# Two-layer decoder trunk on one core: longer planner distances in the first layer's mixers, and the dense block's last down products in another order

## The chip, the cores and the metric

The kernel runs on one core of one Trainium2 chip. The metric is the device time of one execution in microseconds (us). Three runs of the kernel before gave 674.22, 690.02 and 671.63 us; their median is 674.22 us.

## The reference, cut to what matters

256 tokens of width 1024 go through two layers. In each layer one projection feeds three groups of heads, whose outputs are joined and projected back; then come a layer norm, a feed-forward block and another layer norm. The feed-forward block is a dense SwiGLU in the first layer and a top-2-of-8 mixture of experts in the second. All values are float32.

```python
for layer in range(2):
    u, rq, rk, rv, rg, sq, sk, sv = split(x @ w_in[layer])
    y_ssm = s5_mixer(u, ...)              # diagonal complex scan, gelu, gated unit, norm of each group
    y_ret = retention_mixer(rq, rk, rv, rg, ...)   # 8 heads: rotary q and k, decayed scores, norm, silu gate
    y_sb  = stick_breaking_mixer(sq, sk, sv, ...)  # 4 heads: exp(z - cumulative sums), norm
    x = layer_norm(ALPHA * x + concat(y_ssm, y_ret, y_sb) @ w_out[layer])
    f = swiglu(x) if layer == 0 else moe_swiglu(x)
    x = layer_norm(ALPHA * x + f)
```

## The kernel before

**Main products.** Every float32 weight tile is split into a high part (`wh`, ScalarE, line 376) and a low part (`wl`, VectorE, line 378, a few on GpSimd), and each product is made of three TensorE products (`mm3`). Five pairs of split tiles are held (`NHL`), and a tile of a later block is split when an earlier one is done. In layer 0 the input blocks come in the order sv, rv0, u, sq, sk, rq0, rq1, rk0, rk1, rv1, rg0, rg1. A block is 48 TensorE products over two weight tiles of 24; u begins with the 97th product, rq0 with the 241st, and the last one of rg1 is the 576th. Then comes the product with `w_out`, eight row tiles in the order `OUT_ORDER`, the first two of which take the scan mixer's output.

**Lanes.** The mixers are Python generators (`s5_pre`, `s5_main`, `sb_lane`, `ret_lane`) in a planner, the class `Lanes`. The main loop calls `L.tick(1300)` after every 12 products (another count in some blocks), which advances the planned time, and each lane whose time has come then writes its next step, in the order in which the lanes were added: `s5_pre`, `s5_main`, `sb_lane`, `ret_lane`. `yield 2600` so means that the next step is written two ticks, 24 products, later. The planner's numbers are distances in program order and no waits on the chip. TensorE takes its instructions in the order written, save that the tile framework may place a step some products later when by its own estimate the operands are not there. On the chip, an engine works through its queue in order.

**The mixers' steps.** `s5_pre` makes the scan's tables: the powers `xext` (lines 578 to 581), `vmat` (591 to 598), the bank `g` (608 to 611, 64 small products in the trace), `tmat` (614 to 623) and four groups of transposes for `wmat` (625 to 636); `while not pe_open[l]` holds `g` back until block sk is through. `s5_main` makes two banks from `wmat` (`bre` and `bim`, lines 666 to 669), works on VectorE and GpSimd up to the scan (673 to 693), takes the product with `vmat` (695 to 697), copies `yc` out in 16 pieces that alternate between VectorE and ScalarE (699 to 709), and ends with gelu, the `glu` product (715 to 717), sigmoid, a square, the product for its norm (727) and the split into `mT_h`, `mT_l` (732). `sb_lane` goes twice through scores, triangle products (`sb_s`), value products (`sb_a`) and norm (`hd_q`); `ret_lane` goes four times through scores, value products and norm. The functions of ScalarE that need a table are chained in the order written (`fn`).

Before `w_out` the kernel drains the lanes; by the planner's arithmetic only `ret_lane` is then left, and its last steps are written one behind the other.

**The dense block's end.** `DOWN_AFTER[9]` is `[16, 17, 18, 19]`: four row tiles of `ffn_w_down` are multiplied after the last gate and up products, first for tokens 0 to 127 and then for the others, in two column halves `h`. The operands of rows 18 and 19, `f_h` and `f_l` (lines 1075 to 1080), come from the last gate and up products. The layer norm of a token half follows its four row tiles.

Of the kernel before, what the change touches and what calls it, by code (L numbers as in the profile page):

```python
# [226 lines left out]
Y2 = 6000  # L227
Y3 = 2500
# [7 lines left out]
def trunk(ctx, tc, I, out, dbg=None, layers=2):  # L236
# [232 lines left out]
    def s5_pre(l, mp, q, E):  # L469
# [134 lines left out]
                        P["d"].unsqueeze(2).to_broadcast([128, 8, 32]), op=OP.mult)  # L604
        while not pe_open[l]:
            yield 500

        g = Bank()
        for p in range(8):
# [16 lines left out]
        for c in range(2):  # L626
            for h in range(2):
                b = Bank()
                for p in range(4):
                    b.tr(b.t[:, p * 128:(p + 1) * 128], X[:, c, 4 * h + p].rearrange("p a b -> p (a b)"), ident)  # L630
                dst = Wm[:, c, 4 * h:4 * h + 4, :].rearrange("p a b -> p (a b)")
                if h:
                    S.activation(dst, b.t[:], AF.Copy)
                else:
                    V.tensor_copy(dst, b.t[:])
                yield 300
        P.update(V=Vt, T=Tm, W=Wm, tab=tab, R=R)
        S5P[l] = P
        yield 0
# [21 lines left out]
    def s5_main(l, mp, U, mT_h, mT_l):  # L661
        while l not in S5P:
            yield 500
        P = S5P[l]
        tab, R, Wm, Vt, Tm = P["tab"], P["R"], P["W"], P["V"], P["T"]
        bre, bim, y = Bank(), Bank(), Bank()
        for b, c in ((bre, 0), (bim, 1)):
            for p in range(8):
                b.mm_cols(b.t[:, p * 64:(p + 1) * 64], Wm[:, c, p, :], U[:, p, :])
        tc_, ts_ = (tab[:, c, :, 0:64] for c in range(2))  # L670
        tm = mp.tile([128, 4, 512], F32, name="s5t", tag="t8")
        z = mp.tile([128, 2, 512], F32, name="s5z", tag="t4a")
        V.tensor_tensor(tm[:, 0], tc_, bre.t[:], op=OP.mult)
        V.tensor_tensor(tm[:, 3], ts_, bre.t[:], op=OP.mult)
        V.tensor_tensor(tm[:, 1], ts_, bim.t[:], op=OP.mult)
        V.tensor_tensor(tm[:, 2], tc_, bim.t[:], op=OP.mult)
        G.tensor_tensor(z[:, 0], tm[:, 0], tm[:, 1], op=OP.add)
        G.tensor_tensor(z[:, 1], tm[:, 2], tm[:, 3], op=OP.subtract)
        yv = y.t[:].rearrange("p (a b) -> p a b", a=8)
        for p in range(8):  # L680
            y.mm_cols(yv[:, p, :], Tm[:, p].rearrange("p a b -> p (a b)"), U[:, p, :])
        Rf = R.rearrange("p a b -> p (a b)")
        zs = mp.tile([128, 2, 512], F32, name="s5s", tag="t4b")
        for c in range(2):
            V.tensor_tensor_scan(zs[:, c], Rf, z[:, c], 0.0, OP.mult, OP.add)  # L685
        E_ = mp.tile([128, 2, 8, 64], F32, name="s5e", tag="t4a")
        Ef = E_.rearrange("p a b c -> p a (b c)")
        V.tensor_tensor(tm[:, 0], tc_, zs[:, 0], op=OP.mult)
        G.tensor_tensor(tm[:, 3], ts_, zs[:, 0], op=OP.mult)
        V.tensor_tensor(tm[:, 1], ts_, zs[:, 1], op=OP.mult)  # L690
        G.tensor_tensor(tm[:, 2], tc_, zs[:, 1], op=OP.mult)
        V.tensor_tensor(Ef[:, 0], tm[:, 0], tm[:, 1], op=OP.subtract)
        V.tensor_tensor(Ef[:, 1], tm[:, 2], tm[:, 3], op=OP.add)
        yield 11000
        for p in range(8):
            for c in range(2):
                y.mm_cols(yv[:, p, 1:64], Vt[:, c, p].rearrange("p a b -> p (a b)"), E_[:, c, p, 0:63])
        yield 500
        yc = mp.tile([128, 2, T], F32, name="s5y", tag="t2a")
        yp = y.t[:].rearrange("p (h q c) -> p h q c", h=2, q=4)  # L700
        dv = yc.rearrange("p h (c j) -> p h c j", j=4)
        for j in range(4):
            for q in range(4):
                src = yp[32 * j:32 * j + 32, :, q, :]
                dst = dv[32 * q:32 * q + 32, :, :, j]
                if (j + q) % 2:
                    S.activation(dst, src, AF.Copy)  # L707
                else:
                    V.tensor_copy(dst, src)  # L709
        dump(f"s5y{l}", yc)  # L710
        g = mp.tile([128, 2, T], F32, name="s5g", tag="t2b")
        fn(g, yc, AF.Gelu_apprx_tanh)
        yield 4000
        b = Bank()
        for m in range(2):
            for k in range(2):
                b.mm(b.t[:, m * T:(m + 1) * T], P["glu"][:, k, m * 128:(m + 1) * 128], g[:, k, :])
        sg = mp.tile([128, 2, T], F32, name="s5sg", tag="t2c")
        for m in range(2):
            fn(sg[:, m], b.t[:, m * T:(m + 1) * T], AF.Sigmoid, bias=P["glu_b"][:, m:m + 1])  # L720
        o = mp.tile([128, 2, T], F32, name="s5o", tag="t2a")
        V.tensor_tensor(o, g, sg, op=OP.mult)
        sq = mp.tile([128, 2, T], F32, name="s5q", tag="t2c")
        S.activation(sq, o, AF.Square)
        yield 2500
        b = Bank()
        rs = rms_rstd(mp, b, slice(0, 512), sq.rearrange("p a b -> p (a b)"), C["blk16"], "t2b", 1)
        for m in range(2):
            V.scalar_tensor_tensor(o[:, m], o[:, m], P["norm_w"][:, m:m + 1], rs[:, m * T:(m + 1) * T],
                                   op0=OP.mult, op1=OP.mult)  # L730
        dump(f"s5o{l}", o)
        split2(mT_h[:, 0:2, :], mT_l[:, 0:2, :], o)
        yield 0

    def sb_lane(l, mp, qT, kT, v, mT_h, mT_l):
        P = PV[l]
        for ct in range(2):
            zb = [Bank(), Bank()]
            for h in range(2):
                pr = slice(64 * h, 64 * h + 64)  # L740
                zb[h].mm(zb[h].t[:, 0:256], kT[pr, ct, 0:128], qT[pr, ct, :])
                zb[h].mm(zb[h].t[:, 256:384], kT[pr, ct, 128:256], qT[pr, ct, 128:256])
            sm = mp.tile([128, 2, 384], F32, name="sb_s", tag="h3", bufs=3)
            e = mp.tile([128, 2, 384], F32, name="sb_e", tag="h3", bufs=3)
            for h in range(2):
                z = zb[h].t[:, 0:384]
                S.activation(e[:, h], z, AF.Abs)
                fn(e[:, h], e[:, h], AF.Exp, scale=-1.0)
                fn(e[:, h], e[:, h], AF.Ln, bias=b_one)
                V.scalar_tensor_tensor(sm[:, h], z, 0.0, e[:, h], op0=OP.max, op1=OP.add)  # L750
                dv = sm[:, h].rearrange("p (b n) -> p b n", b=3)[:, 0:3:2, :]
                G.affine_select(dv, dv, pattern=[[0, 2], [1, 128]], compare_op=OP.is_gt, fill=0.0, base=0,
                                channel_multiplier=-1)
            yield Y2
            A = mp.tile([128, 2, 384], F32, name="sb_a", tag="h3", bufs=3)
            for h in range(2):
                z = zb[h]
                z.mm(z.t[:, 256:384], C["ntri"], sm[:, h, 256:384])
                z.mm(z.t[:, 0:256], C["ntri"], sm[:, h, 0:256])
                z.mm(z.t[:, 128:256], C["nones"], sm[:, h, 256:384])  # L760
                fn(A[:, h], z.t[:, 0:384], AF.Exp)
                dv = A[:, h].rearrange("p (b n) -> p b n", b=3)[:, 0:3:2, :]
                G.affine_select(dv, dv, pattern=[[0, 2], [1, 128]], compare_op=OP.is_gt, fill=0.0, base=0,
                                channel_multiplier=-1)
            yield Y3
            o = Bank()
            av(o, A, v, 2 * ct)
            sq = mp.tile([128, T], F32, name="hd_q", bufs=2)
            S.activation(sq, o.t[:, 0:T], AF.Square)
            yield 1000  # L770
            rs = rms_rstd(mp, o, slice(T, 2 * T), sq, C["blk64"], "hd_rs")
            on = mp.tile([128, T], F32, name="hd_o", bufs=2)
            V.scalar_tensor_tensor(on, o.t[:, 0:T], P["sb_w"][:, ct:ct + 1], rs, op0=OP.mult, op1=OP.mult)
            split2(mT_h[:, 6 + ct, :], mT_l[:, 6 + ct, :], on)
            dump(f"sb{l}{ct}", on)
            yield 0
# [6 lines left out]
    def ret_lane(l, mp, qT, kT, v, sg, mT_h, mT_l):  # L783
        P = PV[l]
        for ct in range(4):
# [15 lines left out]
            av(o, A, v[ct // 2], 2 * (ct % 2))  # L801
            sq = mp.tile([128, T], F32, name="hd_q", bufs=2)
            S.activation(sq, o.t[:, 0:T], AF.Square)
            yield 1000
            rs = rms_rstd(mp, o, slice(T, 2 * T), sq, C["blk64"], "hd_rs")
            on = mp.tile([128, T], F32, name="hd_o", bufs=2)
            V.scalar_tensor_tensor(on, o.t[:, 0:T], P["gn_w"][:, ct:ct + 1], rs, op0=OP.mult, op1=OP.mult)
# [199 lines left out]
    def ffn(l, fp):  # L1007
# [78 lines left out]
                    router_operands(l + 1, fp)  # L1086
                    pre[l + 1] = L.add(pre[l + 1])
            for t in range(2):
                for h in range(2):
                    for j in DOWN_AFTER[9]:  # L1090
                        down(j, (t,), (h,), last=False)
                pe_open[1] = t == 1
                LNL[t] = L.add(L.urgent(ln(t, acc[t], lnw[:, 0], lnw[:, 1], fp), t == 0))
                L.tick(0)
# [472 lines left out]
```

## Time and profile before

| what | value |
|---|---|
| median of three runs | 674.22 us |
| the profiled execution's own time | 674.3 us |
| its span, first to last instruction | 672.6 us |
| mean granted TensorE clock | 0.979 of full speed |
| TensorE busy | 632.4 us, 94% |
| VectorE busy | 371.5 us, 55% |
| ScalarE busy | 301.6 us, 45% |
| GpSimd busy | 167.1 us, 25% |

The share of busy time is a mean over stages. A matmul's end is modelled and overlaps with the next one, so that the distance of two starts, and not the listed duration, is what a product costs. In a line of the timeline the first number is the start in us from the span's start, the second the time to the end of the line's instructions, and the square bracket the time for which the engine stood idle before it, with the instruction that released it.

### The profile page before, as it was taken

To read this page: it belongs to the slowest core of one execution; us is meant where nothing else is said; L and a number is where in the kernel's file an instruction comes from. 1 tells how busy PE (TensorE), PEld (TensorE's weight loads), DVE (VectorE), ACT (ScalarE), POOL (GpSimd) and SP (SyncE) were. 2 spreads that over 40 slices of the span, in tenths; PEclk is the share of its full clock that TensorE was granted. 3 is DMA by queue.
4 is the path that set the end of the run, shared out by engine and by line. 5 is a ranking of instruction groups with operands and counts; after the bars stand their busy time and mean duration, and the time that the engine had idled before them with its cause. 6 is when DMAs were issued, how large, how long until landed. Compare 5 with 4: busy or idle time off the path is not lost.

```text
span 672.6 us, 14222 instructions
## 1 busy us (share of the span) xinstructions
PE 632.4 (94%) x5652; PEld 500.0 (74%) x5652; DVE 371.5 (55%) x617; ACT 301.6 (45%) x484; POOL 167.1 (25%) x195
## 2 busy tenths in 40 slices
PE   5979889999999999999899998999899999999992
PEld 5978778679899999999799988878655544445542
DVE  5999866568576555555587864764830240012216
ACT  5655589557344444444355579852412200211102
POOL 1651650369998000000150342200000000000001
PEclk9979999999999999999899999999799999999997
DMA  8845155338555555555335241684099999999961
GB/s 323 308 152 161 63 173 179 119 118 288 196 189 188 188 188 188 188 190 187 126 126 189 95 157 63 236 315 194 6 390 335 409 409 352 417 413 414 414 262 67
DMA packets 38309, 150.87 MB, mean 224 GB/s; under 512 B 4640, under 2 KB 4768, under 8 KB 38240
## 3 DMA queue, kind: packets, MB, share of 16 engines
q1 hardware_dynamic: 38096, 149.64, 61.0%
q8 instruction: 49, 0.80, 0.5%
q10 hardware_dynamic: 144, 0.26, 0.1%
q14 instruction: 20, 0.16, 0.1%
HBM read 148.84 MB, written 1.05 MB: 223 GB/s over the span
## 4 chain that ended last, share of the span: by engine, by line
PE 71%; DVE 10%; ACT 9%; issue 5%; POOL 2%; DMA 1%; SPq 0%; DVEq 0%; POOLq 0%; ACTq 0%
PE bank L281 69%; DVE wl L378 3%; ACT wh L376 2%; PE bank L290 2%; ACT r_sw L937 2%; DMA st<-in_w_in_dram 1%; ACT L273 1%; ACT s5y L707 1%; POOL wl L378 1%; ACT L268 1%; DVE s5s L685 1%; ACT rstd L273 1%; DVE s5y L709 1%; DVE tv L579 0%; DVE xext L581 0%
## 5 line engine op out<-in xcount | busy, mean ns | idle before, releaser
L378 DVE TENSOR_TENSOR wl<-st,wh 128x1024 fp32r<-128x1024 f32 (+1 forms) x121 | 156.5, 1296 | 95.5 <-ACT wh L376 95.4
L376 ACT ACTIVATE wh<-st 128x1024 fp32r<-128x1024 f32 (+3 forms) x131 | 136.0, 1045 | 120.8 <-PE bank L281 100.3
L281 PE MATMUL bank<-xth,wh 128*128 128x256 f32 x608 | 174.1, 286 | 0.0
L281 PE MATMUL bank<-xtl,wh 128*128 128x256 f32 x608 | 171.8, 283 | 0.0
L281 PE MATMUL bank<-xth,wl 128*128 128x256 f32 x608 | 171.5, 282 | 0.0
L281 PEld LDWEIGHTS bank<-xth,wh 128*128 128x128 f32 x608 | 115.0, 189 | 2.0 <-issue 0.9
L281 PEld LDWEIGHTS bank<-xth,wl 128*128 128x128 f32 x608 | 115.3, 190 | 0.7 <-issue 0.5
L281 PEld LDWEIGHTS bank<-xtl,wh 128*128 128x128 f32 x608 | 115.1, 189 | 0.8 <-issue 0.2
L281 PE MATMUL bank<-ch,xe 128*32 128x344 f32 (+1 forms) x1280 | 94.2, 453 | 0.0
L281 PEld LDWEIGHTS bank<-ch,xe 128*32 128x32 f32 x1280 | 40.9, 110 | 50.0 <-issue 49.3
L378 POOL TENSOR_TENSOR wl<-st,wh 128x1024 fp32r<-128x1024 f32 (+1 forms) x10 | 21.5, 2176 | 124.8 <-ACT wh L376 124.8
L281 PE MATMUL bank<-ch,hT 128*32 x720 | 52.3, 451 | 0.0
L281 PEld LDWEIGHTS bank<-ch,hT 128*32 128x32 f32 x720 | 23.1, 110 | 27.9 <-issue 27.9
L281 PE MATMUL bank<-wh,xth 128*128 128x256 f32 (+1 forms) x112 | 30.4, 312 | 6.9 <-ACT wh L376 6.8
L281 PE MATMUL bank<-wh,f_h 128*128 128x512 f32 x88 | 35.8, 407 | 0.0
L281 PE MATMUL bank<-wl,f_h 128*128 128x512 f32 (+1 forms) x88 | 35.7, 406 | 0.0
L281 PE MATMUL bank<-wh,f_l 128*128 128x512 f32 x84 | 33.9, 406 | 1.7 <-DVE f_l L415 1.7
L1475 DVE TENSOR_TENSOR hs<-m_s,bank 128x344 f32<-128x344 f32 x10 | 5.1, 513 | 54.6 <-PE bank L281 54.1
L1499 DVE SCALAR_TENSOR_TENSOR y<-bank,gs,y 128x344 fp32r<-128x344 f32 (+1 forms) x15 | 8.6, 573 | 46.1 <-ACT y L1498 46.0
L1498 ACT ACTIVATE y<-bank,gs 128x344 fp32r<-128x344 f32 (+1 forms) x15 | 8.2, 546 | 50.4 <-PE bank L281 50.1
L1473 POOL MEMSET hs<- 128x200 f32 x2 | 0.5, 264 | 120.6 <-PE bank L290 74.2
L281 PE MATMUL bank<-wh,xtl 128*128 128x256 f32 (+1 forms) x112 | 29.0, 300 | 0.2 <-DVE xtl L415 0.2
(304 smaller groups left out, 1013.9 us busy)
## 6 DMA issues: line engine op xcount, KB each, us to landing
st<-in_w_in_dram SPq DMA_DIRECT2D x47, 512.0 KB, 3.7
ch<-in_moe_w_gate_dram SPq DMA_DIRECT2D x32, 688.0 KB, 8.9
ch<-in_moe_w_up_dram SPq DMA_DIRECT2D x32, 688.0 KB, 7.6
ch<-in_moe_w_down_dram SPq DMA_DIRECT2D x24, 688.0 KB, 13.5
st<-in_ffn_w_down_dram SPq DMA_DIRECT2D x21, 512.0 KB, 3.3
st<-in_ffn_w_gate_dram SPq DMA_DIRECT2D x20, 512.0 KB, 3.2
st<-in_ffn_w_up_dram SPq DMA_DIRECT2D x20, 512.0 KB, 3.2
st<-in_w_out_dram SPq DMA_DIRECT2D x16, 512.0 KB, 3.8
```

The costliest lines, as they stand in the source:

```text
L268: chained(S.preload_act_table_set("natural_log_exp_and_others"))
L273: chained(S.activation(out, in_, func, **kw))
L281: PE.matmul(o, lhsT, rhs, start=part not in self.begun, stop=True, skip_group_check=True)
L290: PE.transpose(o, i, ident)
L376: S.activation(hv, st, AF.Copy)
L378: x = (G if on_pool else V).tensor_tensor(lv, st, hv.bitcast(F32), op=OP.subtract)
L685: V.tensor_tensor_scan(zs[:, c], Rf, z[:, c], 0.0, OP.mult, OP.add)
L707: S.activation(dst, src, AF.Copy)
L709: V.tensor_copy(dst, src)
L937: S.activation(sw[32 * i:32 * i + 32], bv[32 * (i ^ 1):32 * (i ^ 1) + 32], AF.Copy)
L1498: S.activation(y[:wb, 0, j, 0:w], a, AF.Copy, scale=gs[:wb, j:j + 1])
L1499: V.scalar_tensor_tensor(y[:wb, 1, j, 0:w], a, gs[:wb, j:j + 1], y[:wb, 0, j, 0:w].bitcast(F32), op0=OP.mult, op1=OP.subtract)
```

## The change

In layer 0 alone seven distances become longer: 2600 in front of the bank `g`, 1200 behind the transposes of `wmat`, 1300 between `bre` and `bim`, 2600 and 1000 in the second pass of `sb_lane` (in front of the triangle products and of the value products), and 1000 in front of the norms' products of `sb_lane` and of `ret_lane`. In the dense block's end the row tiles 16 and 17 are taken for both column halves, then 18 and 19 for both.

```diff
@@ s5_pre
         while not pe_open[l]:
             yield 500
+        if l == 0:
+            yield 2600
 
         g = Bank()
...
                 yield 300
+        if l == 0:
+            yield 1200
         P.update(V=Vt, T=Tm, W=Wm, tab=tab, R=R)
@@ s5_main
         for b, c in ((bre, 0), (bim, 1)):
+            if l == 0 and c:
+                yield 1300
             for p in range(8):
@@ sb_lane
-            yield Y2
+            yield Y2 + 2600 * (1 - l) * ct
             A = mp.tile([128, 2, 384], F32, name="sb_a", tag="h3", bufs=3)
...
-            yield Y3
+            yield Y3 + 1000 * (1 - l) * ct
             o = Bank()
             av(o, A, v, 2 * ct)
             sq = mp.tile([128, T], F32, name="hd_q", bufs=2)
             S.activation(sq, o.t[:, 0:T], AF.Square)
-            yield 1000
+            yield 1000 + 1000 * (1 - l)
@@ ret_lane
-            yield 1000
+            yield 1000 + 1000 * (1 - l)
@@ ffn
             for t in range(2):
-                for h in range(2):
-                    for j in DOWN_AFTER[9]:
-                        down(j, (t,), (h,), last=False)
+                for js in (DOWN_AFTER[9][:2], DOWN_AFTER[9][2:]):
+                    for h in range(2):
+                        for j in js:
+                            down(j, (t,), (h,), last=False)
```

## Rows read from the trace of the kernel before

**Rows 1.** Timeline of TensorE (PE), 19 to 52 us: main products, bank `g`, first scores.
```profile
19.96 0.28 PE L281 MATMUL bank<-xth,wh 128*128 128x256 f32 x1
...
38.45 0.28 PE L281 MATMUL bank<-xth,wl 128*128 128x256 f32 x1
41.16 0.31 PE L281 MATMUL bank<-prm,xext 128*64 128x32 f32 x4 [2.44 <-DVE xext L580]
42.05 0.31 PE L281 MATMUL bank<-cneg,xext 128*64 128x32 f32 x4 [0.58 <-DVE xext L581]
...
43.00 0.33 PE L281 MATMUL bank<-cneg,xext 128*64 128x32 f32 x4
...
45.21 1.66 PE L281 MATMUL bank<-sb_sq,sb_sk 64*128 64x256 f32 x8 [0.60 <-ACT sb_sk L921]
...
51.14 0.60 PE L290 MATMUL bank<-cst,xext 128*128 128x128 f32 x4
```

**Rows 2.** Busy time by stretch, granted clock (PEclk), DMA share, GB/s.
```profile
43.00:50.00 7.00, 6.40 (x57) 5.88 (x55) 6.83 (x13) 4.84 (x11) 0.79 (x2) 0.51 0.26 79
20.00:92.00 72.00, 61.80 (x643) 58.55 (x642) 68.39 (x104) 42.95 (x71) 42.26 (x51) 0.95 0.48 164
```

**Rows 3.** Timeline of ScalarE (ACT) at 44 us, the copy that the first scores need.
```profile
44.56 0.60 ACT L921 ACTIVATE sb_sk<-bank 128x512 f32<-128x512 f32 x1
```

**Rows 4.** Timeline of VectorE (DVE) at 45 us, the low part of rq0's second tile.
```profile
45.78 1.22 DVE L378 TENSOR_TENSOR wl<-st,wh 128x1024 fp32r<-128x1024 f32 x1
```

**Rows 5.** Timeline of TensorE, 62 to 125 us: mixers' products and the first of `w_out`.
```profile
62.06 1.15 PE L281 MATMUL bank<-s5u,wmat 128*64 128x64 f32 x32 [0.52 <-ACT tmat L621]
...
64.96 1.15 PE L281 MATMUL bank<-s5u,wmat 128*64 128x64 f32 x32 [1.08 <-ACT wh L376]
...
81.74 1.14 PE L281 MATMUL bank<-sb_s,cst 128*128 128x128 f32 x6 [2.47 <-POOL sb_s L752]
...
85.62 2.09 PE L281 MATMUL bank<-s5e,vmat 128*64 128x63 f32 x64
...
91.59 1.22 PE L281 MATMUL bank<-sb_a,sb_v 128*64 128x256 f32 x8 [2.28 <-POOL sb_a L763]
...
95.09 0.70 PE L281 MATMUL bank<-hd_q,cst 128*128 128x256 f32 x2 [0.67 <-ACT hd_q L769]
...
97.14 0.93 PE L281 MATMUL bank<-rrq,rrk 64*128 64x256 f32 x8
...
106.68 0.70 PE L281 MATMUL bank<-hd_q,cst 128*128 128x256 f32 x2 [0.95 <-ACT hd_q L803]
...
124.71 0.50 PE L281 MATMUL bank<-wh,mth 128*128 128x512 f32 x1
```

**Rows 6.** Timeline of VectorE, the scan mixer's low part for `w_out`.
```profile
114.90 0.69 DVE L415 TENSOR_TENSOR mtl<-s5o,mth 128x512 fp32r<-128x512 f32 x1
```

**Rows 7.** Timeline of ScalarE, 103 to 114 us: a table load, the sigmoid, the silu.
```profile
103.80 0.40 ACT L414 ACTIVATE mth<-hd_o 128x256 fp32r<-128x256 f32 x1
104.22 1.28 ACT L273 ACT_TABLE_LOAD   x1
105.52 0.84 ACT L273 ACTIVATE s5sg<-bank,small 128x256 f32<-128x256 f32 x2
...
113.54 0.60 ACT L273 ACTIVATE vg<-bank 128x512 f32<-128x512 f32 x1
```

**Rows 8.** Timeline of TensorE, 325 to 334 us: the dense block's last down products.
```profile
325.32 0.39 PE L281 MATMUL bank<-wh,f_h 128*128 128x512 f32 x1
...
326.49 0.40 PE L281 MATMUL bank<-wh,f_l 128*128 128x512 f32 x1
...
329.25 0.50 PE L281 MATMUL bank<-wh,f_l 128*128 128x512 f32 x1 [1.69 <-DVE f_l L415]
...
329.81 0.61 PE L281 MATMUL bank<-wl,f_h 128*128 128x512 f32 x1
...
333.20 0.42 PE L281 MATMUL bank<-wh,f_h 128*128 128x512 f32 x1
```

## The prediction

> **What bounds the kernel now.** I read the page first: TensorE is busy nearly throughout, so what can be won is its idle time and the stretches at the lower clock, where each product costs twice as much. The list of TensorE's waits came next, then its timeline wherever a wait of layer 0's mixers or of the dense block's end stood. Seven waits belong to the groups that the change moves away: 2.44 and 0.58 us in front of bank `g` [rows 1], 0.52 and 1.08 in front of `bre` and `bim`, 2.47 in front of the second triangle products, 2.28 in front of the second value products, 0.67 and 0.95 in front of two norms [rows 5]. An eighth, 1.69 us, is the down products' [rows 8]. Behind the first, the clock goes from 2.4 to 1.2 GHz: it stood at 0.51 of full in 43 to 50 us [rows 2]. The 155 main products from 19.96 to 38.45 us give 0.119 us for one at full speed [rows 1]. The last thing to see is that TensorE is not alone: VectorE was busy 68.39 of the 72 us from 20 to 92 [rows 2], so a product moved here may meet another late operand.
>
> **Where the steps go.** The planner's arithmetic, followed through yields and ticks, gives each step a place, counted in main products of the input blocks. Before and after: first scores of `sb_lane` 252 and 252, bank `g` 252 and 276, transposes 276 to 312 and 300 to 336, `bre` 324 and 360, `bim` 324 and 372, second scores 360 and 372, second triangle products 420 and 456, their value products 444 and 492, their norm 456 and 516, first retention scores 468 in both, first retention norm 504 and 516, product with `vmat` 432 and 480, `glu` 492 and 540, the scan mixer's norm 516 and 564. `w_out` follows the 576th in both. No instruction is added except one load of a ScalarE table, below; no DMA moves against another.
>
> **Part 1, bank `g`.** The wait of 2.44 + 0.58 us was for `xext`. With `g` 24 products later, the first scores are next. They need the copy of sk, which ScalarE ended at 44.56 + 0.60 = 45.16 us [rows 3], and rq0's second tile, the products behind the 264th, needs a low part that VectorE ended at 45.78 + 1.22 = 47.00 [rows 4]. Neither hangs on `g`; both queue behind `xext` and the copies of u, which the change leaves alone. So I take the idle time to stay and to be put down to `sb_sk` or `wl`, and the clock to fall as before. Passing the 264th at 47.0, TensorE does 12 products at the low clock, 12 x 0.238 = 2.9 us, then `g`, whose groups of four are 0.119 us apart (eight steps from 42.05 to 43.00) [rows 1], 16 of them 1.9 us at full speed: 51.7 us. Before, the same place, the first transposes, was reached at 51.14 [rows 1]. Cost 0.6 us. Bounds: with `g` still at the low clock another 1.9 us, 2.5 in all; if VectorE's queue is put in another order and nothing is late, a gain of 2.44 + 0.58 + 0.60 and of 7 x 0.49 = 3.4 us of clock, 7.0 in all.
>
> **Part 2, `bre` and `bim`.** Their 0.52 + 1.08 us go: `wmat`'s last transposes stand 24 products, 2.9 us, ahead of `bre` instead of 12. Gain 1.6, at least 0.
>
> **Part 3, the second pass of `sb_lane`.** Scores and triangle products are 84 products apart instead of 60: 2.9 us of cover against the 2.47 us. What is late there is VectorE's step at line 750, which stands behind the scan in the queue; the scan now starts where the scores do and can still stand before it. Gain 2.5, at least 0. The value products get 12 products and the first retention scores between, 1.4 + 0.9 us [rows 5], against 2.28; each norm 1.4 us against 0.67 and 0.95. Gain 3.9, at least 0.
>
> **Part 4, what is late next.** The scan mixer's end moves by 48 products towards `w_out`. From the `vmat` product to the first `w_out` product it was 124.71 - 85.62 = 39.1 us [rows 5]. Off go 48 x 0.119 = 5.7, the retention scores that now stand ahead of it, 0.9, and the 3.9 us of waits gained in part 3: 28.6 us are left. The mixer's own path, from the `vmat` product over copies, gelu, `glu`, sigmoid, square and norm to the split, took from 85.62 to 114.90 + 0.69, that is 30.0 us [rows 5, 6]. Its sigmoid is now written behind rg0's silu, and chained functions keep that order: one more table load, 1.28 + 0.02 us, and the silu's 0.60 [rows 7] come into the path, 31.9 us. So 3.3 us come back as a wait at `glu`, at the mixer's norm or at `w_out`. Bounds: none, if so much of the 30.0 us was waiting for other work of ScalarE and VectorE; 6.7, if the idle time lowers the clock for as long as in part 1 (3.4 us).
>
> For this load the Trainium skill (ScalarE: Activation LUTs, "What ACT_TABLE_LOAD costs") gives 2.66 us for a switch of table, the load and a drain of 1.38 us. The trace does not agree: the load began 0.02 us behind the end of the instruction before it and the sigmoid 0.02 us behind the load [rows 7]. By the page the path would be 1.4 us longer and the time, an estimate, 1.4 us above the forecast; I go by the rows.
>
> **Part 5, the down products.** From 325.32 to 326.49 five steps took 1.17 us, 0.234 each. The first `f_l` product that waits stood eighth behind 325.32 and was released at 329.25 [rows 8]. Now 14 products stand ahead of it, so TensorE reaches it at 325.32 + 14 x 0.234 = 328.6 and waits 0.65 us: 1.0 won. Behind the old wait eight products took 333.20 - 329.81 = 3.39 us where 8 x 0.234 = 1.87 do [rows 8], the lower clock; I take the shorter idle time not to lower it: 1.5 won. The layer norm's first half starts later, but its two VectorE steps still fit beside the last six products, 1.4 us, of the other half. Gain 2.5, between 0 (the operand later still) and 3.2.
>
> **The sum.** -0.6 + 1.6 + 2.5 + 3.9 - 3.3 + 2.5 = 6.6 us. All that comes behind, the experts' weight stream included, starts from these products and shifts with them. The profiled execution took 674.3 us, its span 672.6, within 0.1 of the median: 674.3 - 6.6 = **667.7 us**.
>
> **The rivals.**
> *The first stall goes too.* If copy and low part are placed earlier, part 1 gives 7.0 instead of -0.6: 660.1 us. For it: block sk's products were through before 38.45 us [rows 1], 6 us ahead of the copy. Against: nothing in the change touches what is queued ahead of them. Chance 0.13.
> *The waits only move.* VectorE, 68.39 of 72 us busy [rows 2], sets the pace up to 92 us, and each wait taken away turns up at another step; the mixers give nothing and part 5 alone stays: 671.8 us. For it: VectorE's share. Against: most waits lie at 81 us and later, with other engines' names on them. Chance 0.22.
> *The scan mixer's end becomes the path* (slower). Its in-order copies and table loads stand between the `vmat` product and `w_out`, now with 28.6 us of cover. If its path grows by 10 us over the 30.0, with new table switches and retention's squares in between, the wait is 13.3 and the lost clock 3.4, 16.7 instead of 3.3: 681.1 us. It decides the sign from a cost of 9.9 us on, which is a path of 35.1 with the clock lost. For it: the path runs over two engines that alternate 16 times. Against: part of the 30.0 was waiting for work that now comes earlier. Chance 0.08.
>
> **How the numbers follow.** The forecast has 0.57, the rivals 0.43. The worst ends of all parts together give -9.2 us, the best 18.2; they hardly meet. The range 661 to 674 holds the forecast and the second rival and leaves out the slow one and most of the first, under 2 in 10. Two per cent, about what a measurement of this kernel can tell from no change, is 13.5 us. Faster by more (under 660.8): half of the first rival and a little of the forecast, 0.09. Slower by more (over 687.7): 0.02. Within: 0.89.
>
> **What would show it.** Right: idle time in front of the first scores or of rq0's second tile at 39 to 47 us, with the clock at half up to about 50; no idle in front of `bre`, the second triangle products and the second norm; some microseconds at `glu`, the scan mixer's norm or the first `w_out` product; `w_out` beginning near 120.6 us instead of 124.7; full clock through the down products. Wrong: full clock at 43 to 50 us; no new wait from 95 to 125 us; or waits at the first retention scores, whose operands pass through the same full VectorE queue.

## The result, and the profile after

The changed kernel takes **678.7 us**, the median of four runs from 678.31 to 679.21, against 674.94 for the kernel before in the same job: 1.0078 times as long, 95% interval 1.0051 to 1.0104. Now and then an execution of any kernel takes some per cent longer (690.02 us among the four of the kernel before), and the ratios leave such executions out. The forecast was 667.7. The profiled execution took 678.31 us, its span 676.6, so 4.0 us more than the span before.

TensorE's timeline, layer 0's mixers and `w_out`; the rows answer to [rows 1, 5]:

```profile
44.98 1.66 PE L281 MATMUL bank<-sb_sq,sb_sk 64*128 64x256 f32 x8 [5.94 <-ACT sb_sk L927]
...
87.53 1.15 PE L281 MATMUL bank<-sb_s,cst 128*128 128x128 f32 x6 [3.48 <-POOL sb_s L758]
88.91 2.08 PE L281 MATMUL bank<-sb_s,cst 128*128 128x128 f32 x6 [0.23 <-POOL sb_s L758]
95.24 1.49 PE L281 MATMUL bank<-rrq,rrk 64*128 64x256 f32 x8 [2.31 <-POOL rrk L945]
...
120.42 1.12 PE L281 MATMUL bank<-s5q,cst 128*128 128x512 f32 x2 [2.28 <-ACT s5q L730]
127.33 0.50 PE L281 MATMUL bank<-wh,mth 128*128 128x512 f32 x1
...
144.85 0.50 PE L281 MATMUL bank<-wh,mth 128*128 128x512 f32 x1 [2.17 <-ACT wh L376]
146.11 0.50 PE L281 MATMUL bank<-wl,mth 128*128 128x512 f32 x1 [0.76 <-DVE wl L378]
```

Seven of the nine waits of [rows 1, 5] are gone. The other two have grown, at the first scores from 0.60 to 5.94 us and at the second triangle products from 2.47 to 3.48, and two new ones stand at the first retention scores (2.31) and the scan mixer's norm (2.28). Added up over every line from 36 us to the first `w_out` product, TensorE was idle for 11.83 us before (the nine waits and 0.24 us at 83.12) and for 14.24 now. The idle time has moved, and it has grown by 2.4 us. That product starts 2.6 us later (127.33 against 124.71). The windows show the clock, columns as in [rows 2]:

```profile
43.00:50.00 7.00, 5.02 (x24) 4.63 (x25) 6.83 (x14) 5.18 (x12) 0.56 (x2) 0.59 0.25 79
88.00:92.00 4.00, 3.77 (x17) 3.35 (x16) 2.91 (x4) 2.73 (x5) 1.17 (x2) 0.58 0.49 144
96.00:99.00 3.00, 3.00 (x17) 2.71 (x15) 2.27 (x3) 0.94 (x1) 3.00 (x4) 0.52 0.71 236
146.00:150.00 4.00, 3.89 (x10) 3.12 (x11) 1.45 (x3) 0.00 (x0) 3.84 (x9) 0.58 0.40 131
330.00:345.00 15.00, 14.46 (x78) 11.99 (x77) 11.58 (x16) 6.05 (x10) 5.08 (x3) 1.00 0.30 106
```

Behind the waits at 87.5 and 95.2 us the clock goes to its lower level, 1.2 GHz. In the trace of the kernel before it did not go down between 80 and 130 us. By the granted clock that costs 4 x 0.42 + 3 x 0.48 = 3.1 us of products. Idle time and clock together are 5.5 us, so 2.9 us must have come back elsewhere ahead of `w_out`: two norm products (0.6 us) now stand behind its first product and not ahead of it; the rest is not broken down.

From the first `w_out` product to the layer norm behind it another 4.6 us are lost: GpSimd's low parts there end at 163.42 against 156.23, 7.2 late. The idle time of that stage is 3.12 us against 0.79, the clock is low from 146 to 150 (4 x 0.42 = 1.7 us), and the two norm products make up the rest. Only the dense block gives something back:

```profile
336.46 0.50 PE L281 MATMUL bank<-wh,f_l 128*128 128x512 f32 x1 [0.54 <-DVE f_l L415]
```

The wait is 0.54 us instead of 1.69 [rows 8] and the clock stays at 1.00 from 330 to 345 us; before, eight products behind the wait took 3.39 us at the lower level [rows 8]. The lag goes from 7.2 to 4.0 us, which is the change of the span.

### The profile page after: what moved, and what is told of

Its sections match the earlier page's. It is cut to its first block, busy times and chain, and to the rows that moved or that the text cites. A ratio compares the mean times of both kernels' runs of the same rounds, so it can differ in the third digit from the quotient of the medians.

```text
span 676.6 us, 14231 instructions
## 1 busy us (share of the span) xinstructions
PE 632.5 (93%) x5652; PEld 501.5 (74%) x5652; DVE 369.4 (55%) x617; ACT 303.0 (45%) x485; POOL 168.8 (25%) x195
## 4 chain that ended last, share of the span: by engine, by line
PE 69%; DVE 10%; ACT 8%; issue 6%; POOL 4%; DMA 1%; SPq 0%; DVEq 0%; POOLq 0%; ACTq 0%
PE bank L281 68%; DVE wl L378 2%; ACT wh L376 2%; PE bank L290 2%; ACT r_sw L943 1%; DMA st<-in_w_in_dram 1%; POOL s5w L497 1%; ACT L273 1%; POOL wl L378 1%; ACT s5y L713 1%; POOL r_sw L944 1%; ACT L268 1%; ACT rstd L273 1%; DVE s5s L691 1%; DVE s5y L715 0%
```

## Where the waits went

VectorE's timeline of the changed kernel, 78 to 90 us: the scan, then `sb_s` (the operand of the second triangle products), then the rope step of rk0:

```profile
78.77 3.42 DVE L691 TENSOR_TENSOR_SCAN s5s<-rdec,s5z 128x512 f32<-128x512 f32 x2 [2.02 <-POOL s5z L683]
...
86.44 1.01 DVE L756 SCALAR_TENSOR_TENSOR sb_s<-bank,sb_e 128x384 f32<-128x384 f32 x2
...
88.51 0.67 DVE L941 TENSOR_TENSOR rrk<-rope,bank 128x512 f32<-128x512 f32 x1
```

The same steps before:

```profile
70.82 2.29 DVE L685 TENSOR_TENSOR_SCAN s5s<-rdec,s5z 128x512 f32<-128x512 f32 x1 [0.86 <-POOL s5z L677]
...
80.66 1.01 DVE L750 SCALAR_TENSOR_TENSOR sb_s<-bank,sb_e 128x384 f32<-128x384 f32 x2
```

Before, too, the scan stood ahead of `sb_s`, and rk0's rope step was at 82.72. With `bre` and `bim` 36 and 48 products later the scan starts 8 us later, and what stands behind it in the queue is 6 us later.

ScalarE's timeline, 140 to 146 us, in the `w_out` stage:

```profile
140.51 0.21 ACT L517 ACTIVATE s5w<-s5w 128x8 f32<-128x8 f32 x1 [3.84 <-POOL s5w L513]
...
143.74 1.79 ACT L376 ACTIVATE wh<-st 128x1024 fp32r<-128x1024 f32 x2
```

The weights' copies for TensorE stand behind layer 1's table functions, the first of which waits for GpSimd. The same functions stood there before:

```profile
133.86 0.21 ACT L517 ACTIVATE s5w<-s5w 128x8 f32<-128x8 f32 x1 [3.27 <-POOL s5w L513]
```

They are now 6.7 us later, `w_out` only 2.6.

## The experiments

Each time is compared with runs of the kernel before on the same chip, given as a ratio; by the job above the changed kernel has 1.0078. "Before +" and "after +" say which kernel was edited; the distances are called scan (in front of `g`, `bre`, `bim`) and heads (second pass of `sb_lane`, both norms).

**One part alone.** Before + the down order:

> The kernel before with the down products' new order alone. If this part did what its step in the prediction says, the wait of 1.69 us falls to about 0.5 and the clock stays up behind it: 2.5 to 3.3 us faster than before, near 671.5 us. If the order only moves the wait to the layer norm behind it: no difference.

0.9962 [0.9928, 0.9996], and 0.9951 [0.9932, 0.9971] in a second set:

> The new order of the down products alone, once more, on the same chip as the two versions with the vmat product 24 products later, to tell what of their gain is its own: 672 to 673.5 us by the term of 2.5 us. Theory (the distances are worth 1 to 2 us more): 1 to 2 us slower than the version with both. Rival (they are worth nothing): as fast as that.

Part 5 holds by itself, with 2.6 to 3.3 us. Before + the scan distances:

> The kernel before with the scan mixer's three distances alone (2600, 1200, 1300). Theory of the late scan: VectorE's long scan steps start some 8 us later and stand ahead of the second scores' step and of the rope steps in its queue, the mixer's end comes close to w_out, and the change's loss is all here: 6 to 11 us slower than before, 680 to 685 us. Rival, the late heads: the four longer distances of the heads do the harm by crowding the products near w_out: this kernel within 2 us of before.

1.014 [1.0088, 1.0191]: 9.5 us slower, more than the whole change. Its trace has the long wait behind the scan at another place than the changed kernel's. `sb_s` stands ahead of the scan here, and TensorE doesn't wait for it. But rk0's rope step on VectorE stands behind the scan's last additions, ScalarE's copies behind that step, and the second exponential of `sb_a` behind these copies, 8 us after its triangle products (ScalarE, then TensorE):

```profile
87.34 2.39 ACT L943 ACTIVATE r_sw<-bank 32x512 f32<-32x512 f32 x4 [6.15 <-DVE rrk L941]
89.76 0.49 ACT L273 ACTIVATE sb_a<-bank 128x384 f32<-128x384 f32 x1
```

```profile
91.50 1.54 PE L281 MATMUL bank<-sb_a,sb_v 128*64 128x256 f32 x6 [5.16 <-POOL sb_a L769]
```

Before + the head distances, then those with the down order:

> The kernel before with the four heads' distances alone (2600 and 1000 in the second pass of the stick-breaking lane, 1000 in front of the norms). Theory of the late scan: the scan steps stand early as before, the four waits of 2.47, 2.28, 0.67 and 0.95 us go: 3 to 6 us faster, 668 to 671 us. Rival, the late heads: 4 to 8 us slower.

> The changed kernel without the scan mixer's three distances. Theory of the late scan: both gains add, 6 to 9 us faster than before, 665 to 668 us. Rival, the late heads: about as slow as the changed kernel, 676 to 680 us.

1.0021 [0.998, 1.0063] and 0.997 [0.9935, 1.0004]. The heads win nothing alone, and with the down order no more than that order. The second of these is the changed kernel without the scan distances, so taking those out gives back some 7 us (0.997 against 1.0078). In the trace with the heads alone the removed waits come back, most of them at one place, `glu`: TensorE's idle time up to `w_out` is 11.95 us, as before, and the clock is 0.57 from 96 to 104 us. ScalarE's queue (first fence) and TensorE's (second):

```profile
97.54 0.39 ACT L707 ACTIVATE s5y<-bank 32x128 f32<-32x128 f32 x1 [0.45 <-DVE s5y L709]
97.94 1.28 ACT L273 ACT_TABLE_LOAD   x1
99.24 0.63 ACT L273 ACTIVATE s5g<-s5y 128x512 f32<-128x512 f32 x1
...
101.18 0.87 ACT L273 ACTIVATE sb_a<-bank 128x384 f32<-128x384 f32 x2
```

```profile
87.33 1.14 PE L281 MATMUL bank<-sb_s,cst 128*128 128x128 f32 x6 [1.05 <-POOL sb_s L752]
...
99.92 3.78 PE L281 MATMUL bank<-s5g,prm 128*128 128x256 f32 x8 [5.17 <-ACT s5g L273]
```

The exponentials of `sb_a` could start at 88.5 us, behind the triangle products. They start at 101.18, behind the copies of y and the gelu. Before, they ran ahead of these copies, which began at 92.15:

```profile
87.68 0.87 ACT L273 ACTIVATE sb_a<-bank 128x384 f32<-128x384 f32 x2
```

**Half of the scan distances.** Before + only `g`; before + only `bre` and `bim`:

> The kernel before with the longer distance in front of bank g alone (24 products). Theory (the scan goes late): the idle time in front of g only moves to the first scores (5.8 us behind the copy of sk, against 2.44 + 0.58 + 0.60 before), and the scan mixer's bre and bim move from the 324th to the 348th product, half of the way that all three distances move them. All three alone cost 9.2 us; so this one costs about half, 3 to 6 us: 678 to 681 us against 675, with the second triangle or value products waiting 2 to 5 us at 82 to 92 us. Rival 1 (only the bre/bim distances hurt): 675.5 us, the waits at 82 to 92 us as before, 2.47 and 2.28. Rival 2 (the distance of g carries all of it): 683 to 685 us.

> The kernel before with the two distances in front of bre and bim alone (12 products each: bre from the 324th to the 336th, bim to the 348th). Theory (the scan goes late): the 0.52 and 1.08 us in front of bre and bim go, the 2.44 + 0.58 + 0.60 us in front of g and the first scores stay; the scan starts some 2 to 3 us later and stands in VectorE's queue ahead of the second scores' step: the second value products wait 4 us or more instead of 2.28, the low clock behind them. 676 to 679 us against 675. Rival 1 (as the prediction had it, these waits are simply won): 673.4. Rival 2 (the distance of g is harmless and these two carry all 9.2 us): 683 to 685.

1.0141 [1.0091, 1.019] and 1.0163 [1.0108, 1.0218]. Either half costs as much as the whole, so my sharing out by products was wrong. With `g` alone the first scores wait 6.00 us, and the second triangle products:

```profile
86.86 3.79 PE L281 MATMUL bank<-sb_s,cst 128*128 128x128 f32 x12 [6.63 <-POOL sb_s L754]
```

With `bre` and `bim` alone TensorE's wait for `sb_s` is 7.39 us at 84.48, and VectorE shows its cause:

```profile
81.54 0.69 DVE L696 TENSOR_TENSOR s5e<-s5t 128x512 f32<-128x512 f32 x1
...
82.47 0.55 DVE L754 SCALAR_TENSOR_TENSOR sb_s<-bank,sb_e 128x384 f32<-128x384 f32 x1
```

In both, `bim` is at the 348th product, 12 in front of the second scores, and apart from one 0.42 us step the scan's end is the last that VectorE finishes ahead of `sb_s`. So a distance does not cost by its length: `sb_s` stands behind the scan before, in these two and in the changed kernel, with 2.47, 6.63, 7.39 and 3.48 us of waiting, and with all three scan distances alone it is `sb_a` that comes late. Much of the price is the clock: up to `w_out` TensorE's idle time is only 3.9 us (`g`) and 1.8 us (`bre` and `bim`) above the 11.83 before, but the clock was at half behind these waits (0.51 from 85 to 92 us; 0.50 from 80 to 90) and again near `w_out` (0.50 from 126 to 139; 0.51 and 0.50 from 124 to 134).

**The place in VectorE's queue.** After, with the scan emitted 12 products later:

```
         zs = mp.tile([128, 2, 512], F32, name="s5s", tag="t4b")
+        if l == 0:
+            yield 1300
```

> The changed kernel with the scan itself emitted 12 products later, so that the second scores' step (sb_s, first half) stands in VectorE's queue ahead of the scan's four multiplications and additions (82.12 to 86.44 us) and no longer behind them; the vmat product and the scan mixer's end go 12 products further. Theory (the scan went ahead of the second scores' step, and that is the wait of 3.48 us): this wait falls to under 1 us and the low clock behind it goes, 674 to 676.5 us against 678.7; what the scan mixer's end then lacks is at most 1.5 us. Rival (sb_s waits for POOL's select or ScalarE's exponentials, not for the scan): the wait stays over 2.5 us, 678 to 681.

1.0208 [1.0136, 1.028], far slower than either theory had it:

```profile
84.61 1.14 PE L281 MATMUL bank<-sb_s,cst 128*128 128x128 f32 x6 [1.55 <-POOL sb_s L760]
...
94.14 1.66 PE L281 MATMUL bank<-rrq,rrk 64*128 64x256 f32 x8 [3.72 <-POOL rrk L947]
123.23 2.08 PE L281 MATMUL bank<-s5q,cst 128*128 128x512 f32 x2 [5.39 <-ACT s5q L732]
...
129.72 0.50 PE L281 MATMUL bank<-wh,mth 128*128 128x512 f32 x1 [1.73 <-ACT mth L414]
...
145.07 0.93 PE L281 MATMUL bank<-rrq,rrk 64*128 64x256 f32 x8
```

The wait for `sb_s` falls from 3.48 to 1.55, with 0.73 in place of 0.23 at its second half, so the scan's place was its cause for the larger part. But the retention scores wait 3.72 us instead of 2.31: the two steps together cost 6.0 us, as in the changed kernel, and the idle time has moved once more.

The price is at `w_out`. With 12 products more the scan mixer is not done when the input blocks end. The kernel's `drain` in front of `w_out` (line 958 of the kernel before) then finishes that lane alone, with no products between its last steps: its norm waits 5.39 us and `w_out` 1.73. With no other lane left, as in the kernel before and the changed one, the same line writes out all of `ret_lane`; here the scores of its third and fourth pass stand behind the first `w_out` product, at 135.65 and 145.07. From the first `w_out` product to the first product of the dense block it is 36.2 us instead of 30.2. So this run does not price the scan's place alone.

**The place in ScalarE's queue.** Before + heads and down order, `glu` further from the gelu (`yield 4000` becomes 7900 in layer 0):

> The distances in the second pass of sb_lane and in front of the norms, and the down order, without the scan's three distances, and glu 36 products further from the gelu (the 528th instead of the 492nd). Without the last, these distances won nothing: 5.17 us of waiting for the gelu took the place of those removed, with the clock at 0.54 to 0.61 from 96 to 104 us. Theory (the gain was only handed to glu): with cover in front of glu this wait falls under 1 us and the clock stays up: 666 to 669 us against 675. Rival (the scan mixer's end is the path, as in the prediction's slow rival): the wait is handed on to the scan mixer's norm or to w_out, 4 us or more; 671 to 674.

1.0006 [0.9984, 1.0027]. The wait is handed to the value products, which need the late exponentials:

```profile
102.94 1.71 PE L281 MATMUL bank<-sb_a,sb_v 128*64 128x256 f32 x7 [7.43 <-POOL sb_a L763]
```

Then the cause itself: the `vmat` product later, by 48 or by 24, so that the copies of y are issued behind the exponentials.

```
-        yield 11000
+        yield 11000 + 5200 * (1 - l)     # the other: 2600
```

> The distances in the second pass of sb_lane and in front of the norms and the down order, without the scan's three distances, and the vmat product 48 products later (the 480th, where the change has it) with the scan where the kernel before has it. Without the last, ScalarE's eight copies of y, its gelu and two table loads (91.7 to 101.2 us) stood in its queue ahead of the exponentials of sb_a, whose triangle products were through at 88.5 us; with it the compiled queue has the exponentials first. Theory (ScalarE's queue turned the gain into the wait at glu or sb_a): no wait above 1.5 us from 85 to 105 us, full clock there, 665 to 669 us against 674.5. Rival 1 (the scan mixer's end becomes the path): 3 us or more of waiting at glu, the scan mixer's norm or w_out, 670 to 674. Rival 2 (VectorE's backlog sets the pace, whatever the order): the waits turn up at the retention scores or at rt_a, 673 to 676.

> As the one with 48, but the vmat product only 24 products later (the 456th). The compiled queue of ScalarE has the exponentials of sb_a between the first copies of y, ahead of the gelu. Theory: as there, with the scan mixer's end 24 products further from w_out: 665 to 669 us against 674.5, and no wait at w_out or the scan mixer's norm. Rival 1 (the copies of y, which take turns with VectorE's, hold the exponentials up all the same): 2 to 4 us at sb_a or glu; 670 to 673. Rival 2 (VectorE's backlog): 673 to 676.

With 48: 1.002 [0.9988, 1.0051]; where its gain went is open. With 24: 0.9951 [0.9912, 0.999], and no wait is left at `glu` or `sb_a`. ScalarE's queue, then, made that wait. New ones of 0.98 and 1.69 us stand at the retention's `rt_a`, with the clock at 0.57 from 100 to 104, and two more, 0.56 and 1.56, from 118 to 122. The same without the down order, and with a further 12 products (`yield 1500` becomes 2800 in layer 0) in front of the retention's value products:

> The distances in the second pass of sb_lane and in front of the norms with the vmat product 24 products later, and the old order of the down products. Theory (ScalarE's queue, and the down order's 2.5 us a term of its own): 672.5 to 674 us against 675, that is 1 to 2 us for the distances once the copies of y no longer stand ahead of sb_a's exponentials; the f_l wait is back at 1.69 us. Rival (these distances are worth nothing in any order, all of the gain is the down order's): 675.

> The version with the vmat product 24 products later and the down order, and besides the retention's value products 12 products further from their scores in layer 0. Before, 0.98, 1.69 and 1.56 us of waiting for rt_a stood there, with the clock at 0.57 from 100 to 104 us. Theory (rt_a is late behind VectorE's reduction and copies by less than 3 us): these waits fall under 1 us together and 2 to 4 us are won: 667 to 669 against 671 without it. Rival (VectorE's backlog hands the wait on to the norms or to w_out): 671 to 673.

1.0035 [1.0005, 1.0065] without the down order: the heads with 24 are worth nothing yet. With the retention's distance 0.9904 [0.987, 0.9937], median 668.6 us: **faster than both kernels**, by 6.5 us against the one before, and 2.2 below the median of the down order alone on the same chip (670.83; the two intervals meet between 0.9932 and 0.9937). In its trace the first two of these waits are one of 1.15 us, TensorE's idle time up to `w_out` is 9.21 us, the least of all these kernels, and the window that was slow is at full clock:

```profile
96.00:104.00 8.00, 6.86 (x47) 5.45 (x46) 7.24 (x15) 7.23 (x12) 0.03 (x1) 1.00 0.44 140
```

**The first stall.** After + the copies of u all on ScalarE (the condition at line 910 of the kernel before becomes `l == 0 or (j + q) % 2`):

> The changed kernel with the 16 copies of u (layer 0) all on ScalarE instead of by turns on ScalarE and VectorE. Theory: the copy of sk is late because ScalarE's copies of u wait each for the VectorE copy ahead of it, which stands in VectorE's full queue (4.66 us at 42.3 us). With all of them on ScalarE (16 x 0.27 = 4.3 us from 33.7) the copy of sk ends near 40.5 instead of 45.0: TensorE waits 1 to 2 us in front of the first scores instead of 5.94, and some 1 to 3 us more at rq0's second tile, whose low part VectorE ends near 44.5. Together 2 to 5 us come back and the scan starts so much earlier: 672 to 676 us against 678.7 of the changed kernel. Rival 1 (VectorE's work sets the pace up to 92 us, the copies' place is no matter): the 5.94 us turn up whole at rq0's low part or at bre; 678 to 679. Rival 2 (ScalarE is then late with wh copies): a wait of over 3 us behind wh between 36 and 50 us; 679 to 682.

1.0026 [0.9991, 1.0061], some 3.5 us better than the changed kernel by the two ratios, whose intervals just meet:

```profile
39.48 0.93 PE L281 MATMUL bank<-sb_sq,sb_sk 64*128 64x256 f32 x8
...
47.81 0.31 PE L281 MATMUL bank<-prm,xext 128*64 128x32 f32 x4 [4.47 <-issue]
```

The first scores don't wait any more, so the copy of sk was late because of the copies of u. But the weights' low parts now come first in VectorE's queue, `xext` ends at 48.05 instead of 41.77, and `g` waits. The profile puts that to "issue"; but the half of `xext` that the first of these products reads was ended by VectorE at 47.71, 0.1 us ahead of it.

**VectorE's load.** The `vmat` table on GpSimd (`G` for `E` in lines 592 to 598 of the kernel before), for before + down order, for after, and for after with u on ScalarE:

> The kernel before with the new order of the down products, and layer 0's vmat table (18 instructions, 9.8 us of VectorE between 42.3 and 57.7 us) computed on GpSimd. Theory (VectorE's queue sets the pace of the mixers): with this work out of the queue the waits behind it, 0.60 at the first scores, 0.52 and 1.08 at bre and bim, 2.47 and 2.28 in the second pass of sb_lane, shrink to under 2 us together; the wait for xext stays. 4 to 6 us faster than the down order alone: 667 to 669.5 us against 675. Rival 1 (the waits hang on ScalarE and POOL): vmat's some 13 us on POOL push the selects and the rope products back, the waits grow; 675 to 680. Rival 2 (nothing moves): 673, as the down order alone.

> The changed kernel with layer 0's vmat table on GpSimd. Theory (VectorE's queue): the copies of u come sooner, the first scores wait some 3.5 us instead of 5.94, the scan chain starts some 4 to 6 us earlier, and the 3.48 us at sb_s and 2.31 at the retention scores fall below 1.5 together: 669 to 673 us against 678.7 of the changed kernel and 675 before. Rival 1 (POOL becomes late): sb_s and rrk wait for POOL as long as now or longer, 677 to 682. Rival 2 (the distances themselves cost, whatever VectorE does): 677 to 679.

> The changed kernel with the copies of u on ScalarE and the vmat table on GpSimd. With u on ScalarE alone the first scores did not wait and bank g waited 4.47 us, since VectorE ended xext at 48.05 instead of 42.0; 3.76 us stood at the retention scores; about 4 us faster than the changed kernel. Theory (VectorE's queue): g still waits some 4 us, but behind it 9.8 us of VectorE's work are gone, and sb_s's and rrk's waits with them: 667 to 671 us. Rival (POOL becomes late): rrk waits 4 us or more, 674 to 677.

1.0023 [1.0, 1.0047], 1.0131 [1.0089, 1.0173], 1.0126 [1.0077, 1.0175]: all slower than without. The first selects stand behind the table on GpSimd. Before + down order, GpSimd and then TensorE:

```profile
62.86 0.72 POOL L598 TENSOR_TENSOR vmat<-tv 128x256 f32<-128x256 f32 x1
63.54 0.77 POOL L752 TENSOR_SCALAR_AFFINE_SELECT sb_s<-sb_s 128x256 f32<-128x256 f32 x2
```

```profile
64.00 0.58 PE L281 MATMUL bank<-sb_s,cst 128*128 128x128 f32 x1 [7.09 <-POOL sb_s L752]
```

Past this wait the later ones shrink (0.65 instead of 2.45 us at the second `sb_s`), as VectorE's relief should do. So the test says that the selects come late when GpSimd has the table ahead of them; it does not settle how much VectorE's load alone is worth, and that rival of the queue's order stays open.

**The `w_out` stage.** After, with two of the three steps of layer 1's tables moved into the dense block (`range(3)` becomes `range(1)`):

> The changed kernel with the first ScalarE functions of layer 1's scan tables (two of three steps) moved from in front of w_out's last rows into the dense block. Theory: the 2.17 + 0.76 us of waiting for wh and wl at 145 us, and the low clock at 146.7 to 150 (1.5 to 2 us), come from these functions, which stand ahead of the wh copies in ScalarE's queue and wait 3.84 us for POOL. Without them there both go: 674 to 675.5 us against 678.7. Rival 1 (the copies wait for their weights or for free buffers): the wait stays, 678 to 679. Rival 2 (the functions block as much where they now stand, the relu rows of the dense block, and POOL's table work runs into the low parts): a wait of 2 to 4 us there, 677 to 680.

1.0123 [1.0082, 1.0163]. The 2.17 + 0.76 us and the low clock at 146 to 150 are gone, and the first product behind the stage starts at 152.5 instead of 157.5 us, so these functions were the cause of the loss there. They block again where they now stand:

```profile
180.53 0.50 PE L281 MATMUL bank<-wh,f_h 128*128 128x512 f32 x1 [3.07 <-ACT f_h L414]
215.53 0.58 PE L281 MATMUL bank<-xth,wl 128*128 128x256 f32 x1 [2.62 <-DVE wl L378]
```

## Why the prediction was wrong

The miss in the span is 10.6 us (-6.6 against +4.0): 6.7 up to the first `w_out` product (120.6 predicted, 127.33 measured), 4.6 in the `w_out` stage, and 0.7 the other way in the dense block.

- **Part 1** was right in kind. The idle time went to the first scores, 5.94 us, with the clock at half. `g` ended at 53.0 and not at 51.7 (52.90 for its last start, 0.12 for a step). I had put the 264th product at 47.0, when its operand is there; but the first scores end only at 46.6, and 12 more products stand between. The cost was 1.9, within the bound of 2.5. And a product at the lower clock took 0.213 us (18 steps from 46.95 to 50.79), 1.8 times the 0.119 and not twice, as I had it.
- **Part 2** failed behind the place it looked at. The 0.52 and 1.08 us went, as said, and the distances that removed them made the scan late; on the kernel before they alone cost 11 us (1.0163).
- **Part 3 is the step that failed.** I wrote that "the scan now starts where the scores do and can still stand before it" and priced this at nothing. It does stand before it, as it did before the change, but 8 us later: 3.48 us at `sb_s`, where the 2.47 were to go, and 2.31 at the retention scores, with 3.1 us of clock behind the two. The other 3.9 us (2.28, 0.67, 0.95) went, as said. And I costed the head distances by TensorE's products alone. Their consumers' place in ScalarE's queue changed too, and with the scan in its old place that took the whole gain back (1.0021).
- **Part 4** was right in kind and nearly in size: 2.28 us at the scan mixer's norm against 3.3. The silu and its load stand between the gelu and the sigmoid, as worked out:

```profile
114.25 1.28 ACT L273 ACT_TABLE_LOAD   x1
115.55 0.60 ACT L273 ACTIVATE vg<-bank 128x512 f32<-128x512 f32 x1
...
116.47 1.28 ACT L273 ACT_TABLE_LOAD   x1
```

  Here too the function starts 0.02 us behind the end of the load (114.25 + 1.28, 115.55), and not the 1.38 us later that the Trainium skill (ScalarE: Activation LUTs, "What ACT_TABLE_LOAD costs") adds for a drain. The lost clock that was its bound, 3.4 us, did come, 3.1 us, but behind the waits of part 3.
- **Part 5** was right, 3.2 us against 2.5: the wait of 0.54 stands where 0.65 was worked out, and the clock stays up.
- **Not in the sum at all:** the `w_out` stage, 4.6 us. I took all that comes behind as shifting with the products. ScalarE's table functions for layer 1 shifted by 6.7 us, the products by 2.6.

The prediction speaks of seven waits and lists eight; its sums use all eight.

Of the rivals, "the waits only move" was nearest: 11.83 and 14.24 us of idle time say that they moved and grew. It was priced at 671.8 because I held a moved wait to cost what it cost before. In the changed kernel's trace longer waits between 80 and 130 us took the clock down, where those before had not. But a wait of this length does not settle it: in the trace with the down order alone, whose mixers are written as before, the clock was 0.57 from 81 to 85 us, behind a wait of 2.45 us. The slow rival's mechanism, the scan mixer's end in front of `w_out`, shows with the scan 12 products later than in this change, but there the program order at `drain` changes too.

## What to carry to other kernels

A longer distance on TensorE also moves the place of every consumer in the in-order queues of the other engines. Before pricing a removed wait as a gain, list what then stands ahead of its operand on VectorE, ScalarE and GpSimd, and compare the sums of idle time, not the named waits. Count what the clock adds behind a longer wait. Where two chains share a queue, moving the one that overtakes (here the `vmat` product by 24, then the retention's values by 12) was worth more than widening each wait by itself. And look at what the program writes at fixed places: a lane that is late for one `drain` changes the order of all that follows.

## What the runs showed beside this

With `bre` and `bim` alone, TensorE had waits of 0.56, 0.15, 0.47 and 1.37 us between 119 and 124 us, none long. It was busy for 5.65 of the 8 us from 116 to 124, and behind that the clock was at its lower level, 0.51 in the next 6 us and 0.50 in the 4 behind them:

```profile
116.00:124.00 8.00, 5.65 (x34) 3.10 (x32) 5.82 (x12) 7.93 (x12) 2.11 (x2) 1.00 0.10 22
124.00:130.00 6.00, 5.80 (x16) 2.54 (x16) 1.89 (x7) 2.44 (x4) 0.28 (x1) 0.51 0.31 101
```

No single wait here was long, and the clock fell. And eleven of the copies of u took 3.08 us in a row on ScalarE alone, without a gap; by turns with VectorE one of them left ScalarE idle for 4.16 us in the changed kernel, until VectorE's copy ahead of it was done.
